# S5 layer: u regrouped through DRAM on GpSimd's queue for state inputs on all 128 rows, tables fetched ten steps ahead, twelve gated outputs accumulated over K

## The chip, the core and the metric

The kernel runs on one core of one Trainium2 chip. The metric is the device time of one execution in microseconds, the median of three runs. All engines, queues and lines are those of that core; L157 is line 157 of the kernel before.

## The reference

A trunk of four layers on x of 256 positions by 1024 channels, float32. Layer i mixes tokens with attention (0, 3), a state-space layer (1) or pooling (2); a SwiGLU feed-forward layer (FFN) follows each. The change lies in the state-space layer, S5:

```python
u = (h @ w_in).astype(F32)
u_g = u.reshape(B, S, S5_GROUPS, S5_GROUP).astype(jnp.complex64)
lam_bar = jnp.exp(lam * dt)
b_bar = ((lam_bar - 1.0) / lam)[..., None] * b_mat
bu = jnp.einsum('gpc,bsgc->bsgp', b_bar, u_g)
_, states = lax.associative_scan(combine, (lam_seq, bu), axis=1)
y = jnp.einsum('gcp,bsgp->bsgc', c_mat, states).real.reshape(B, S, D_MODEL)
y = y + d.astype(F32) * u
g = jax.nn.gelu(y).astype(h.dtype)
val, gate = jnp.split(g @ w_glu, 2, axis=-1)
return val * jax.nn.sigmoid(gate)
```

There are 64 groups of 16 channels with 64 complex states each. `combine` is the first-order recurrence s = lam_bar * s + bu.

## The kernel before

**Dense products.** Activations lie transposed, channels on partitions. Each weight unit of 128 x 1024 is fetched by SyncE (SP) into one of four `raw` buffers, then split into a high and a low float32r part: ScalarE copies (L98), VectorE subtracts (L99), into one of five `hl` buffers. `unit` (L102) hands out the next unit; fetches run three units ahead of use, splits two. A dense product of a unit with 8 k-tiles takes 24 matmuls of 128x256 (`term`, L159: high x high, low x high, high x low), all through `mm` (L157). In the FFN of layers 1 to 3 a pair of matmuls of 512 and 256 columns does the same.

**Ticks.** `tick` (L117) counts the dense work: one tick is about six dense matmuls. Other work is put on ticks with `at` and so lands between dense matmuls. A scheduler then sets the order on each engine; engines run their instructions in that order.

**S5.** `s5` (L780) multiplies eight units of w_s5 (m = 0..7, each one block of 128 channels, that is 8 groups). `evict` (L788) scales a product with the norm R (VectorE, L791) into `u`, whose columns are grouped by position modulo 4. `tables` (L833) fetches, on SP's queue, the block's input matrices E (512 KB), the rotation and decay tables tab (384 KB) and the output matrices par (768 KB) from DRAM, where an earlier stage (`prepare`) has written them on GpSimd's queue (lines L712 to L773). `core` (L843) computes the states of four positions at a time:

```python
for ri in range(2):
    for r in range(4):
        for i in range(4):
            rows = slice(32 * i, 32 * i + 32)
            self.mm(e[:, i, 64 * ri:64 * ri + 64], E[rows, ri, r], u[rows, r], r == 0, r == 3)
```

These are the state inputs: 32 matmuls on 32 rows each (K = 32), four row groups i to four PSUM banks, accumulated over r. Each float32 matmul stands as two instructions on TensorE. VectorE then rotates (products A and B with cosine and sine, L862 to L865), scans (L867), rotates back (L870 to L874) into `sx`. `emit` (L877), six ticks later, adds four feedthrough matmuls of u (`KT`, widths 256, 192, 128, 64) and 32 matmuls of `sx` into the outputs of the block; ScalarE applies gelu (L888), and the result is split into G, high and low (L194, L195). Blocks follow each other every five ticks.

**GLU.** Sixteen output tiles of G @ w_glu: a value and a gate for each of eight column tiles d. Those of d = 0 and 1 are accumulated over k while the blocks run, four 128-column products for each G[k], waiting until block k is emitted. The four banks that `e` used are then opened for the other twelve tiles, whose dense products follow one after the other. Each column is gated (sigmoid on ScalarE, product L829, residual L830) and settled: its next-layer X (ScalarE L209, VectorE L210) and its square (L218, L221).

PSUM has eight banks: two named `acc`, two `tp`, and four in a quad that is either `P` or `e`.

## Time and profile before

| what | value |
|---|---|
| median of three runs | 1142.85 us (1141.98 to 1143.46) |
| the profiled execution | 1147.59 us |
| its span, first to last instruction | 1145.8 us |
| TensorE clock granted in it | 0.995 |
| TensorE, VectorE, ScalarE, GpSimd busy | 97%, 76%, 60%, 11% of the span |
| S5 layer in the span | from 335.56 to 444.62 us |

How to read it. A row of the page or of the groups view names the line, the engine, the operation, the tiles out<-in without buffer numbers, the shape and the count, then the busy time, the mean length of one in ns, and the idle time of the engine ahead of it with what ended it. PE is TensorE's matmul side, PEld its weight loads, DVE VectorE, ACT ScalarE, POOL GpSimd. A timeline row gives start and length in us of neighbouring instructions of one kind. A row of DMA issues gives queue, count, size and the median time from issue to landing. Matmuls are pipelined, so starts tell more of their pace than lengths. A stretches row gives, for each stretch, each engine's busy time and instructions, the granted clock, the share of the DMA engines' time in use, and GB/s.

### The profile page before, as it was taken

How to read it: one execution, taken by the hardware profiler on the slowest of the kernel's cores; microseconds unless marked ns; L12 is line 12 of the kernel's file. 1: busy time of each engine (PE TensorE's matmuls, PEld its weight loads, DVE VectorE, ACT ScalarE, POOL GpSimd, SP SyncE). 2: the span in 40 equal slices, each digit the busy share in tenths (PEclk: the TensorE clock that was granted, in tenths of full speed). 3: DMA queues.
4: the chain of work that ended last, by engine and by line, in shares of the span. 5: the costliest groups of instructions: out<-in, count | busy, mean ns of one | idle time of the engine just before them, and what ended most of it. 6: DMA issues, size and time to landing. Idle time of an engine off the chain costs nothing. (4 is left out here: it accounts for less than half of the span.)

```text
span 1145.8 us, 22375 instructions
## 1 busy us (share of the span) xinstructions
PE 1114.2 (97%) x8706; PEld 1025.4 (89%) x8706; DVE 866.6 (76%) x1647; ACT 682.2 (60%) x1273; POOL 130.1 (11%) x167
## 2 busy tenths in 40 slices
PE   6989999999999999999999899999999999999996
PEld 6888999999999999888888888888899898888886
DVE  6898698887969975988756588876656757878663
ACT  6466675777763254766644676665545777666551
POOL 1187000111110000000000000000004730000000
PEclk9999999999999999999999899999999999999999
DMA  8655366786889744765666255556666544655661
GB/s 267 211 188 164 104 228 224 252 269 213 254 329 332 268 140 155 227 195 186 179 179 194 93 179 194 193 179 189 192 200 215 167 145 148 214 184 188 182 188 49
DMA packets 63210, 224.98 MB, mean 196 GB/s; under 512 B 7648, under 2 KB 7984, under 8 KB 62976
## 3 DMA queue, kind: packets, MB, share of 16 engines
q1 hardware_dynamic: 56368, 200.86, 54.6%
q0 software_dynamic: 6160, 22.00, 5.8%
q8 instruction: 68, 1.11, 0.4%
q10 hardware_dynamic: 576, 0.69, 0.2%
q14 instruction: 38, 0.31, 0.1%
HBM read 208.81 MB, written 14.71 MB: 195 GB/s over the span
## 5 line engine op out<-in xcount | busy, mean ns | idle before, releaser
L157 PE MATMUL P<-X,hl 128*128 128x256 f32 (+1 forms) x4560 | 674.9, 307 | 2.8 <-ACT v L327 1.6
L157 PEld LDWEIGHTS P<-X,hl 128*128 128x128 f32 x4560 | 615.1, 189 | 52.0 <-issue 7.2
L99 DVE TENSOR_TENSOR hl<-raw,hl 128x1024 fp32r<-128x1024 f32 (+3 forms) x363 | 434.5, 1199 | 149.7 <-ACT hl L98 141.7
L98 ACT CAST hl<-raw 128x1024 fp32r<-128x1024 f32 (+3 forms) x363 | 371.7, 1028 | 152.6 <-PE acc L157 71.6
L157 PE MATMUL acc<-H,hl 128*128 128x512 f32 (+1 forms) x1628 | 251.6, 315 | 0.0
L157 PEld LDWEIGHTS acc<-H,hl 128*128 128x128 f32 x1628 | 226.8, 188 | 21.1 <-issue 0.8
L183 ACT COPY lo<-P 128x256 f32<-128x256 f32 x126 | 46.6, 371 | 105.6 <-PE P L157 105.6
L184 DVE TENSOR_TENSOR t<-P,lo 128x256 f32<-128x256 f32 x126 | 53.2, 423 | 44.1 <-ACT lo L183 44.1
L411 POOL TENSOR_SCALAR nb<-nb,c 128x128 f32<-128x128 f32 (+1 forms) x64 | 63.9, 1011 | 1.1
L244 POOL TENSOR_TENSOR rs<-rs,mhalf 128x2 f32<-128x2 f32 x9 | 7.3, 810 | 486.6 <-DVE rs L243 486.6
L157 PE MATMUL acc<-X,hl 128*128 128x256 f32 (+1 forms) x384 | 61.6, 301 | 0.2
L157 PEld LDWEIGHTS acc<-X,hl 128*128 128x128 f32 x384 | 50.6, 188 | 3.9 <-DVE X L195 0.3
L432 ACT ACTIVATE pt<-pt,st 128x128 f32<-128x128 f32 (+1 forms) x64 | 28.6, 447 | 26.0 <-DVE st L430 25.8
L279 ACT ACTIVATE t<-t 128x256 f32<-128x256 f32 x88 | 36.8, 418 | 7.7 <-DVE t L278 4.6
L157 PE MATMUL P<-hl,X 128*128 128x336 f32 (+1 forms) x192 | 40.5, 330 | 0.0
L209 ACT ACTIVATE X<-x,gains 128x256 fp32r<-128x256 f32 x55 | 27.7, 505 | 15.1 <-DVE x L264 14.5
L218 ACT ACTIVATE s<-x 128x256 f32<-128x256 f32 x63 | 25.6, 406 | 15.9 <-DVE x L264 13.1
L157 PEld LDWEIGHTS P<-hl,X 128*128 128x128 f32 x192 | 33.4, 197 | 0.0
L157 PE MATMUL acc<-hl,X 128*128 128x352 f32 x96 | 24.4, 338 | 8.7 <-DVE X L207 7.5
L210 DVE SCALAR_TENSOR_TENSOR X<-x,gains,X 128x256 fp32r<-128x256 f32 x56 | 26.7, 479 | 5.7 <-ACT X L209 5.6
L281 DVE TENSOR_TENSOR t<-t 128x256 f32<-128x256 f32 x66 | 27.9, 423 | 1.8
L278 DVE TENSOR_TENSOR t<-t,R 128x256 f32<-128x256 f32 x66 | 27.9, 423 | 1.8
(179 smaller groups left out, 854.8 us busy)
## 6 DMA issues: line engine op xcount, KB each, us to landing
raw<-in_w_gu SPq DMA_DIRECT2D x176, 512.0 KB, 3.9
raw<-in_w_dn SPq DMA_DIRECT2D x64, 512.0 KB, 3.6
raw<-in_w_qk SPq DMA_DIRECT2D x32, 512.0 KB, 3.4
raw<-in_w_dn SPq DMA_DIRECT2D x32, 384.0 KB, 3.2
raw<-in_w_fo SPq DMA_DIRECT2D x16, 512.0 KB, 4.0
raw<-in_w_glu SPq DMA_DIRECT2D x16, 512.0 KB, 5.8
raw<-in_w_vf SPq DMA_DIRECT2D x15, 520.0 KB, 4.4
nb<-nd POOLq DMA_DIRECT2D x24, 256.0 KB, 5.3
```

The source lines that it names most:

```text
L98: nc.scalar.copy(hl[:, 0, s], raw[:, s])
L99: nc.vector.tensor_tensor(out=hl[:, 1, s], in0=raw[:, s], in1=hl[:, 0, s].bitcast(F32), op=ALU.subtract)
L157: return self.nc.tensor.matmul(out, lhsT=lhsT, rhs=rhs, start=start, stop=stop).ins
L183: nc.scalar.copy(lo, o[:, N:])
L184: nc.vector.tensor_tensor(out=t, in0=o[:, 0:N], in1=lo, op=ALU.add)
L209: nc.scalar.activation(self.X[:, d, 0], x, AF.Identity, scale=g)
L210: nc.vector.scalar_tensor_tensor(out=self.X[:, d, 1], in0=x, scalar=g, in1=self.X[:, d, 0].bitcast(F32), op0=ALU.mult, op1=ALU.subtract)
L278: nc.vector.tensor_tensor(out=t, in0=t if wide else G, in1=R, op=ALU.mult)
L279: nc.scalar.activation(t, t, AF.Silu)
L281: nc.vector.tensor_tensor(out=h, in0=h if wide else U, in1=t, op=ALU.mult)
L411: nc.gpsimd.tensor_scalar(out=nb[:, i], in0=nb[:, i], scalar1=self.c[t][:, 4 * n + i:4 * n + i + 1], scalar2=None, op0=ALU.add)
L432: nc.scalar.activation(pt, pt, AF.Exp, bias=st[:, 0:1], scale=-1.0, accum_out=st[:, 1:2])
```

## The change

1. **State inputs.** u is stored to a DRAM scratch `ud[m]` and loaded back as `ue` by four DMAs, one for each position r modulo 4, all on GpSimd's queue. In `ue` the partitions are (r, c) and the columns (i, j), so all four r stand under each other and one matmul of 128 rows does what four of 32 rows did: 8 matmuls a block, into one `tp` bank. The matrices E are laid out to match (`prepare`: XS).
2. **Rotation.** The tables get a fourth row, minus the sine, made by ScalarE per block; the adds and subtracts on halves become one 512-column add each.
3. **Times.** The core of block m stands at tick 22 + 6m (it was 10 + 5m), and 14 ticks after its eviction at least; its tables are fetched ten ticks ahead; E, tab have three buffers, u eight, ue four. `emit` follows after seven ticks.
4. **GLU.** The quad stays `P`. Twelve of the sixteen output tiles (d = 0 to 5) are accumulated over k in six banks, 36 dense matmuls for each G[k], from sixteen units of 768 columns. Only d = 6 and 7 are left for afterwards, from four units of 1024.

```diff
+FIRST_CORE = 22
...
         def evict(m, P):
-            u = mp.tile([128, 4, 64], F32, tag="u", name="u", bufs=4)
+            u = mp.tile([128, 4, 64], F32, tag="u", name="u", bufs=8)
             nc.vector.tensor_tensor(out=u, in0=v(P), in1=v(self.R), op=ALU.mult)
-            self.at(max(1, 10 + 5 * m - self.now + t0), lambda: self.core(m, u, G))
+            nc.gpsimd.dma_start(self.ud[m], u.rearrange("p r j -> p (r j)"))
+            ue = mp.tile([128, 4, 64], F32, tag="ue", name="ue", bufs=4)
+            def load():
+                for r in range(4):
+                    nc.gpsimd.dma_start(ue[32 * r:32 * r + 32],
+                                      self.ud[m].rearrange("(i c) (r j) -> r c i j", i=4, r=4)[r])
+            load()
+            self.at(max(14, FIRST_CORE + 6 * m - self.now + t0), lambda: self.core(m, u, ue, G))
...
-            self.at(1 + 5 * m, lambda m=m: self.tables(m))
+            self.at(max(1, FIRST_CORE + 6 * m - 10), lambda m=m: self.tables(m))
...
-        acc = [self.bank("acc") for _ in range(2)]
+        outs = [self.bank(t) for t in ("P", "P", "P", "P", "acc", "acc")]
         for k in range(8):
             while self.emitted < k + 1:
                 self.tick()
-            if k % 2 == 0:
+            for h in range(2):
                 hl = self.unit()
-            for d in range(2):
-                for h in range(2):
-                    c = (k % 2 * 4 + 2 * d + h) * 128
-                    self.term(acc[d][:, h * N:h * N + N], hl, slice(c, c + 128), G, k, k == 0 and h == 0, k == 7 and h == 1)
-                self.tick()
-        self.open_quad()
+                for d in range(3):
+                    for s in range(2):
+                        c = (2 * d + s) * 128
+                        self.term(outs[3 * h + d][:, s * N:s * N + N], hl, slice(c, c + 128), G, k,
+                                  k == 0 and s == 0, k == 7 and s == 1)
+                    self.tick()
...
-        e = self.p4.tile([128, 4, 512], F32, tag="e", name="e")
+        nc.scalar.activation(tab[:, 3], tab[:, 1], AF.Identity, scale=-1.0)
+        e = self.bank("tp").rearrange("p (a n) -> p a n", a=2)
         for ri in range(2):
-            for r in range(4):
-                for i in range(4):
-                    rows = slice(32 * i, 32 * i + 32)
-                    self.mm(e[:, i, 64 * ri:64 * ri + 64], E[rows, ri, r], u[rows, r], r == 0, r == 3)
+            for i in range(4):
+                self.mm(e[:, ri, 64 * i:64 * i + 64], E[:, ri, i], ue[:, i], True, True)
...
-        nc.vector.tensor_tensor(out=ij(A), in0=ev, in1=ij(c2), op=ALU.mult)
-        nc.vector.tensor_tensor(out=ij(B), in0=ev, in1=ij(s2), op=ALU.mult)
-        nc.vector.tensor_tensor(out=A[:, 0], in0=A[:, 0], in1=B[:, 1], op=ALU.add)
-        nc.vector.tensor_tensor(out=A[:, 1], in0=A[:, 1], in1=B[:, 0], op=ALU.subtract)
+        nc.vector.tensor_tensor(out=A, in0=e, in1=c2, op=ALU.mult)
+        nc.vector.tensor_tensor(out=B, in0=e[:, ::-1], in1=sn, op=ALU.mult)
+        nc.vector.tensor_tensor(out=A, in0=A, in1=B, op=ALU.add)
...
-        self.at(6, lambda: self.emit(m, u, CX, KT, sx, G))
+        self.at(7, lambda: self.emit(m, u, CX, KT, sx, G))
```

In the order, first TensorE where the first blocks' state inputs stand. P and acc are dense products of w_s5, e<-u,E are state inputs, tp<-u,par the feedthrough. Before:

```order
L157 MATMUL P<-X,hl 128x256 x4
L250 MATMUL tp<-cst,rs 128x128 x2
L157 MATMUL P<-X,hl 128x256 x18
L157 MATMUL acc<-X,hl 128x256 x6
L157 MATMUL e<-u,E 128x64 x32
L157 MATMUL acc<-X,hl 128x256 x13
L157 MATMUL e<-u,E 128x64 x32
L157 MATMUL acc<-X,hl 128x256 x23
```

After (tp<-ue,E are the state inputs):

```order
L158 MATMUL P<-X,hl 128x256 x4
L251 MATMUL tp<-cst,rs 128x128 x2
L158 MATMUL P<-X,hl 128x256 x18
L158 MATMUL acc<-X,hl 128x256 x84
L158 MATMUL tp<-ue,E 128x64 x8
L158 MATMUL acc<-X,hl 128x256 x12
L158 MATMUL tp<-ue,E 128x64 x8
L158 MATMUL acc<-X,hl 128x256 x30
L158 MATMUL tp<-u,par 128x256
```

The state inputs of block 0 stood six dense matmuls after the first two units; now 84 stand between, and 12 dense ones between blocks 0 and 1.

GpSimd's queue from the start of the S5 layer to the next transfer it issues (band, for the pooling layer). Before:

```order
L712 DMA s5d7_88<-pk_2433 128x512
L784 MEMSET sx0_4509 128x8
L784 MEMSET sx1_4510 128x8
L244 TENSOR_TENSOR rs_4504<-rs_4504,mhalf_75 128x2
L472 DMA band_6096<-in_band 128x1088
L474 DMA pbs_6098<-in_pool_bs 128x16
```

After (ud0 and ue_4600 are block 0's, ud1 and ue_4608 block 1's, and so on):

```order
L785 MEMSET sx0_4517 128x8
L785 MEMSET sx1_4518 128x8
L245 TENSOR_TENSOR rs_4512<-rs_4512,mhalf_75 128x2
L793 DMA ud0_81<-u_4597 128x256
L793 DMA ud1_82<-u_4605 128x256
L798 DMA ue_4600<-ud0_81 32x4x64 x4
L798 DMA ue_4608<-ud1_82 32x4x64 x4
L793 DMA ud2_83<-u_4644 128x256
L793 DMA ud3_84<-u_4687 128x256
L793 DMA ud4_85<-u_4732 128x256
L798 DMA ue_4647<-ud2_83 32x4x64 x4
L798 DMA ue_4690<-ud3_84 32x4x64 x4
```

The loads of block 0 stand behind the stores of blocks 0 and 1; those of block 2 behind the stores of blocks 2, 3 and 4.

ScalarE around the first gelu (its output is g, tp its input bank). Before:

```order
L98 CAST hl_4744<-raw_4611 128x1024
L98 CAST hl_4865<-raw_4742 128x1024
L98 CAST hl_4943<-raw_4863 128x1024
L888 ACT_TABLE_LOAD
L888 ACTIVATE g_4802<-tp_4765 128x4x64
L98 CAST hl_5070<-raw_4941 128x1024
L194 CAST X_4513<-g_4802 128x256
L888 ACTIVATE g_4917<-tp_4880 128x4x64
L194 CAST X_4513<-g_4917 128x256
```

After (tab_4593, 4671, 4728 and 4842 are the tables of blocks 0 to 3):

```order
L99 CAST hl_4742<-raw_4697 128x1024
L858 ACTIVATE tab_4671<-tab_4671 128x256
L858 ACTIVATE tab_4728<-tab_4728 128x256
L99 CAST hl_4825<-raw_4740 128x768
L99 CAST hl_4868<-raw_4823 128x768
L99 CAST hl_5021<-raw_4866 128x768
L858 ACTIVATE tab_4842<-tab_4842 128x256
L892 ACT_TABLE_LOAD
L892 ACTIVATE g_4914<-tp_4877 128x4x64
L195 CAST X_4521<-g_4914 128x256
```

The negations of the sine (L858) for blocks 0 to 3 stand ahead of the first gelu, with the splits of GLU units between them.

## The prediction

> **What bounds the kernel now.** I read the page first: it says which engine is busy over the whole span.

> ```profile
> PE 1114.2 (97%) x8706; PEld 1025.4 (89%) x8706; DVE 866.6 (76%) x1647; ACT 682.2 (60%) x1273; POOL 130.1 (11%) x167
> ```

> TensorE is busy all the time. The change touches the S5 layer, so I cut that layer out with the stretches view: its first two dense units, the part in which the eight state blocks run, the last twelve dense units, and ten microseconds of heavy loading.

> ```profile
> core 0: us, PE busy (x) PEld busy (x) DVE busy (x) ACT busy (x) POOL busy (x), PEclk, DMA share, GB/s
> 335.56:342.95 7.39, 6.85 (x56) 6.44 (x55) 3.49 (x8) 2.35 (x5) 0.87 (x3) 1.00 0.85 324
> 342.95:411.57 68.62, 67.39 (x1338) 62.88 (x1337) 60.56 (x107) 22.39 (x30) 0.00 (x0) 1.00 0.75 270
> 411.57:444.62 33.05, 33.05 (x283) 33.05 (x281) 24.98 (x39) 19.63 (x33) 0.00 (x0) 1.00 0.52 176
> 340.00:350.00 10.00, 9.28 (x170) 8.72 (x170) 7.06 (x11) 2.37 (x3) 0.51 (x1) 1.00 0.99 379
> ```

> The layer takes 444.62 - 335.56 = 109.06 us, and TensorE idles in 1.8 us of it. VectorE has 8 us to spare in the middle stretch. The timeline of TensorE gives the price of each piece (start, length, instructions; a length overlaps the next start, so I take start to start):

> ```profile
> 338.90 0.61 PE L157 MATMUL tp<-cst,sq 128*128 128x1 f32 x4
> 339.37 0.72 PE L157 MATMUL P<-X,hl 128*128 128x256 f32 x4
> 340.56 0.43 PE L250 MATMUL tp<-cst,rs 128*128 128x128 f32 x2 [0.47 <-POOL rs L244]
> 342.95 0.87 PE L157 MATMUL acc<-X,hl 128*128 128x256 f32 x6
> 344.06 2.01 PE L157 MATMUL e<-u,E 32*128 32x64 f32 x64 [0.24 <-DVE u L791]
> 346.01 1.81 PE L157 MATMUL acc<-X,hl 128*128 128x256 f32 x13
> 352.50 1.31 PE L157 MATMUL tp<-u,par 128*128 128x256 f32 x8
> 353.75 1.10 PE L157 MATMUL tp<-sx,par 128*32 128x64 f32 x64
> 354.78 0.97 PE L157 MATMUL acc<-X,hl 128*128 128x256 f32 x6
> 360.75 0.65 PE L157 MATMUL tp<-sx,par 128*32 128x64 f32 x30 [0.34 <-issue]
> 386.51 0.53 PE L157 MATMUL tp<-sx,par 128*32 128x64 f32 x19 [0.47 <-issue]
> 411.57 33.21 PE L157 MATMUL P<-X,hl 128*128 128x256 f32 x280
> 444.62 0.87 PE L157 MATMUL acc<-X,hl 128*128 128x512 f32 x4
> 445.33 0.87 PE L157 MATMUL P<-X,hl 128*128 128x512 f32 x4
> ```

> A dense matmul costs 33.05/280 = 0.118 us, so the 576 of the layer (192 of w_s5, 384 of the GLU) cost 68.0. A block's state inputs cost 346.01 - 344.06 = 1.95 (eight: 15.6), its outputs 354.78 - 352.50 = 2.28 (eight: 18.2). With 0.47 for the sums and 0.66 for the spread and its wait that is 102.9 of 109.06. Of the other 6.1 us, 1.05 are the three named idles (0.24, 0.34, 0.47); the rest is small change, some 0.1 us wherever dense and state matmuls meet. So there is little waiting for the change to remove.

> **State inputs on the full array: 0.** Before, 64 instructions stand as 16 groups of four that run side by side on 32 rows each: 1.95/16 = 0.12 us a group. After, 8 matmuls are 16 instructions on 128 rows. Nothing in the trace has their exact shape; two rows bracket it. The sums of squares, four instructions of one column, take 339.37 - 338.90 = 0.47, or 0.117 each, although they move almost nothing; what is left to set that pace is the 128 weight columns that each of them loads. The four feedthrough matmuls (eight instructions, 1280 columns) take 353.75 - 352.50 = 1.25, or 0.00098 a column, which would make 64 columns 0.063. I take 0.117, since every one of the 16 loads new weights: 1.9 us a block, as before. Both ends are kept: 0 or 8 x (1.9 - 1.0) = 7.2 us of gain.

> [...]

> **The regrouping: +0.75.** The first state inputs now need u stored to DRAM, loaded back by four DMAs, all on GpSimd's queue. What hides it is dense work moved ahead: by the order 84 dense matmuls stand before them where six stood, so TensorE reaches them at 342.95 + 84 x 0.118 = 352.86. The other side:

> ```profile
> 342.87 1.14 DVE L791 TENSOR_TENSOR u<-P,R 128x256 f32<-128x256 f32 x2 [3.17 <-PE P L157]
> L712 POOL DMA_DIRECT2D s5d<-pk x3 | 1.6, 540 | 16.2 <-DVE pk L528 16.2
> s5d<-pk POOLq DMA_DIRECT2D x8, 256.0 KB, 3.9
> s5d<-pe POOLq DMA_DIRECT2D x16, 256.0 KB, 4.8
> nb<-nd POOLq DMA_DIRECT2D x24, 256.0 KB, 5.3
> dd<-in_s_d POOLq DMA_DIRECT2D x1, 4.0 KB, 8.1
> out_y<-xg SPq DMA_DIRECT2D x2, 256.0 KB, 2.5
> ```

> u of block 0 is there at about 343.5. Its store (128 KB) should land some 4.3 us later, between the two rows of GpSimd's stores, since the DMA engines are 0.99 busy just then: 347.8. GpSimd spends 0.54 on each issue, so the fourth load starts 3 x 0.54 = 1.6 later, at 349.4. A load of 32 KB in pieces of 256 bytes does not occur before; I take 4.2, nearest to GpSimd's short stores: 353.6. TensorE waits 353.6 - 352.86 = 0.75. The ends: 2.5 for each leg gives 350.1, no wait; 5.3 for each gives 355.7, a wait of 2.9; 8.1, a small load queued behind a large one, gives 361.3, a wait of 8.5. The wait is lost whole, since all dense matmuls of the later units stand behind these on TensorE.

> [...]

> Block 1's loads leave GpSimd about 2.2 us after block 0's, and its matmuls come 1.95 + 12 x 0.118 = 3.4 us after: hidden, with 1.2 us to spare. From block 2 on the loads are done microseconds early. GpSimd has nothing else to do there, so nothing queues behind its waits.

> **The sign table on ScalarE: +0.5.** Each block adds a 256-column negation on ScalarE that needs its table landed, while table buffers are three deep. By the order, block 3's negation stands ahead of the gelu of block 0, and its table may only be fetched when block 0's last multiplication has read its own.

> ```profile
> 346.20 0.68 DVE L862 TENSOR_TENSOR A<-e,tab 128x512 f32<-128x512 f32 x1
> 346.80 0.68 DVE L863 TENSOR_TENSOR B<-e,tab 128x512 f32<-128x512 f32 x1
> L867 DVE TENSOR_TENSOR_SCAN A<-tab,A 128x256 f32<-128x256 f32 x16 | 10.1, 674 | 0.0
> L888 ACT ACT_TABLE_LOAD x1 | 1.3, 1283 | 0.0
> L888 ACT ACTIVATE g<-tp 128x256 f32<-128x256 f32 x8 | 5.1, 635 | 27.5 <-PE tp L157 27.5
> tab<-s5d SPq DMA_DIRECT2D x8, 384.0 KB, 5.7
> par<-s5d SPq DMA_DIRECT2D x8, 768.0 KB, 6.9
> ```

> Counted from the start of block 0's state inputs: 2.1 for them, then on VectorE, 0.6 apart as the two first rows are (346.80 - 346.20), five 512-column operations, two scans, and in between block 1's first product and u of block 5 (0.57, half of the pair above): 2.1 + 8 x 0.6 + 0.6 = 7.5. Fetch 5.7, negation 0.4, table load 1.28, gelu 0.64: 15.5. The outputs of block 1 need the PSUM bank that this gelu empties. TensorE is there after state inputs of block 0, 12 dense matmuls, state inputs of block 1, 30 dense, outputs of block 0, 6 dense, state inputs of block 2, 6 dense, with 0.1 where the kind changes: 1.95 + 1.5 + 1.95 + 3.6 + 2.4 + 0.8 + 2.0 + 0.8 = 15.0. A wait of 0.5. With par's 6.9 it is 1.7; with a table that lands in 4 us, none.

> **Twelve outputs over K, and the end: -0.65 + 0.4 + 0.3.** Between blocks there are now 36 dense matmuls for 30: 36 x 0.118 + 1.95 + 2.28 + 0.3 of changes make 8.8 us a block. VectorE has six 512-column operations and two scans (4.8), G's split (0.4) and two splits of 768 columns (three quarters of the 1.22 below, 1.8): 7.0, so it stays behind TensorE. The wait for u (0.24) goes, and about half of the 0.81 us of "issue" idle, since 48 fewer weight loads and matmuls are issued per block: -0.65. Two blocks' outputs are split round dense work: +0.4. The DMAs of a block are 1.70 MB of tables, 0.79 of weights, 0.26 of u, in 8.8 us 313 GB/s, against the 379 moved at a share of 0.99: hidden, since tables and weights are fetched a block or more ahead; without that lead every block would wait. At the end six columns are settled at once while TensorE has 96 dense matmuls, 11.3 us:

> ```profile
> L99 DVE TENSOR_TENSOR hl<-raw,hl 128x1024 fp32r<-128x1024 f32 x26 | 31.7, 1221 | 7.3 <-ACT hl L98 7.0
> L830 DVE TENSOR_TENSOR x<-x,s 128x256 f32<-128x256 f32 x8 | 3.3, 422 | 0.2
> ```

> VectorE needs 6 x 4 x 0.42 = 10.1 and five splits, 6.1, so 16.2; three columns start up to 3.5 us early, and the FFN asks for the last X only 7/8 of 32 x 0.355 (445.33 - 444.62 holds two pairs) = 9.9 us into it. Only the bank of column 5 is tight: 0 to 1.5, I take 0.3.

> **Sum.** 0 + 0.75 + 0.5 - 0.65 + 0.4 + 0.3 = +1.3 us. The profiled execution took 1147.59 us (span 1145.8, 1.8 around it), so it would take 1148.9. The median of the runs lies 4.7 below that execution, and the difference carries over: 1142.85 + 1.3 = 1144.1.

> **Rivals.** (1) *The round trip is hidden*: both legs land within 3.9 us. Then 1.3 - 0.75 = +0.55, without the sign table's wait +0.05: 1142.9, no change. For it: pk's 3.9. Against: the DMA share of 0.99. [...] (2) *Faster*: the full-array matmuls go at the pace of their columns, 7.2 less: 1136.9. For it: the feedthrough's 0.063; against: 0.117 for one column. [...] (3) *Slower*: the first block's loads queue behind the tables, which in this order are fetched for three blocks in one burst. From 4.75 us a leg on, the wait passes 1.75 and the total 2.3; at 8.1 a leg it is 1.3 + 7.8 = +9: 1151.9; at 6 a leg, +4.9: 1147.7. For it: nb's 5.3 and pe's 4.8; against: a store of half that size, loads of an eighth.

> **Chances.** Below 0.2% (2.3 us) no measurement of this kernel tells a change. The forecast has 0.42, within 1142 to 1146; rival 1 0.18; rival 2 0.10, and 0.02 that all small idles go; rival 3 0.28. Faster is 0.12. Slower is rival 3 and a little of the forecast's upper end, 0.30. The same is the rest, 0.58. The range leaves out rival 2 and the far end of rival 3: 1140.8 to 1148.5.

> **What would show it.** Right: the state-input pieces still take 1.9 us; one wait at the first of them, of 0 to 3 us, named after ue's DMA; a short wait before block 1's feedthrough, named after the gelu; the layer still about 110 us. Wrong: state inputs near 1 us; waits at later blocks; TensorE starved by splits at the start of the FFN.

## The result: slower, and the profile after

The changed kernel takes 1150.61 us (median of 4 runs, 1150.13 to 1151.03); beside it the kernel before took 1143.15 (4 runs). The ratio is 1.0052, 95% interval 1.0036 to 1.0067. In a second series it was 1.0055 (1.0041 to 1.0069). The forecast was 1144.1, with a range to 1148.5.

The lines of the changed kernel lie one higher than before, from L780 on a few more: the matmuls are L158, the eviction of u is L792, the store L793, the loads L798. The profiled execution took 1150.36 us. Its page begins like that of before: TensorE is at work for 97% of the span, only with fewer instructions.

```profile
PE 1114.8 (97%) x8322; PEld 1028.4 (90%) x8322; DVE 866.9 (75%) x1635; ACT 684.0 (60%) x1285; POOL 151.4 (13%) x207
```

So the share of busy time says nothing of the loss. The waits of TensorE in the S5 layer and at the start of the FFN say where it is (engine, line, tile, releaser; total, times, longest):

```profile
PE tp L158 <- DMA ue<-ud: 4.2, 1, 4.2
PE tp L158 <- DVE sq L222: 1.6, 1, 1.6
PE tp L251 <- POOL rs L245: 1.0, 2, 0.6
```

The third was there before. The first two are new. Here are the first state inputs in TensorE's timeline, and a block in the steady part:

```profile
350.73 1.00 PE L158 MATMUL acc<-X,hl 128*128 128x256 f32 x7
355.92 3.65 PE L158 MATMUL tp<-ue,E 128*128 128x64 f32 x16 [4.18 <-DMA ue<-ud]
359.32 2.91 PE L158 MATMUL acc<-X,hl 128*128 128x256 f32 x12
362.03 2.03 PE L158 MATMUL tp<-ue,E 128*128 128x64 f32 x16
...
379.10 1.89 PE L158 MATMUL tp<-ue,E 128*128 128x64 f32 x16
380.80 0.95 PE L158 MATMUL acc<-X,hl 128*128 128x256 f32 x6
```

Two things are to be seen. TensorE stands still for 4.18 us until the first block's `ue` has landed. And then the first block takes 359.32 - 355.92 = 3.40 us where a later one takes 380.80 - 379.10 = 1.70; the twelve dense products behind it take 2.71, where 12 x 0.118 = 1.4. The stretches view tells why: the granted clock is at half for 6.83 us, from just ahead of the end of the wait. The second row is the layer, the third the FFN behind it.

```profile
core 0: us, PE busy (x) PEld busy (x) DVE busy (x) ACT busy (x) POOL busy (x), PEclk, DMA share, GB/s
334.22:444.86 110.64, 105.92 (x1289) 103.49 (x1288) 84.85 (x132) 45.08 (x73) 22.77 (x43) 0.97 0.76 260
444.86:634.40 189.54, 187.39 (x1099) 164.19 (x1098) 138.48 (x221) 110.38 (x187) 1.83 (x3) 1.00 0.60 186
352.06:355.47 3.41, 0.00 (x0) 0.00 (x0) 0.00 (x0) 0.00 (x0) 1.56 (x4) 1.00 0.89 278
355.47:362.30 6.83, 6.38 (x30) 6.41 (x31) 2.01 (x4) 1.66 (x2) 5.72 (x11) 0.50 0.52 138
```

How long the legs of the round trip took stands in the DMA issues from 342 to 352.9 us (size, median us from issue to landing). The DMA share there is 1.02, and the weights beside them need 12.4 us:

```profile
raw<-in_w_glu SPq DMA_DIRECT2D x2, 384.0 KB, 12.4
ud<-u POOLq DMA_DIRECT2D x2, 128.0 KB, 6.0
ue<-ud POOLq DMA_DIRECT2D x8, 32.0 KB, 5.4
```

The second wait is on VectorE's account. In its timeline at the start of the FFN it stands still for 2.34 us ahead of a product of 128x8, the pooling bias and scale of layer 2, whose table comes over GpSimd's queue. X and squares of the columns d = 6 and 7 are behind it, and so the sums:

```profile
448.51 0.43 DVE L839 TENSOR_TENSOR x<-x,s 128x256 f32<-128x256 f32 x1
451.27 0.17 DVE L476 TENSOR_TENSOR pbs<-pbs 128x8 f32<-128x8 f32 x1 [2.34 <-DMA pbs<-in_pool_bs]
451.36 0.48 DVE L211 SCALAR_TENSOR_TENSOR X<-x,gains,X 128x256 fp32r<-128x256 f32 x1
```

### The profile page after: what moved, and what is told of

Read it like the earlier page. It is cut to its first block, busy times and chain, and to the rows that moved or that the text cites. A ratio compares the mean times of both kernels' runs of the same rounds, so it can differ in the third digit from the quotient of the medians.

```text
span 1148.6 us, 21710 instructions
## 1 busy us (share of the span) xinstructions
PE 1114.8 (97%) x8322; PEld 1028.4 (90%) x8322; DVE 866.9 (75%) x1635; ACT 684.0 (60%) x1285; POOL 151.4 (13%) x207
## 5 line engine op out<-in xcount | busy, mean ns | idle before, releaser
L158 PE MATMUL P<-X,hl 128*128 128x256 f32 (+1 forms) x4512 | 672.1, 308 | 1.3 <-ACT y L504 1.3
L158 PEld LDWEIGHTS P<-X,hl 128*128 128x128 f32 x4512 | 611.7, 189 | 50.1 <-issue 7.2
L100 DVE TENSOR_TENSOR hl<-raw,hl 128x1024 fp32r<-128x1024 f32 (+3 forms) x367 | 435.8, 1190 | 145.7 <-ACT hl L99 137.5
L99 ACT CAST hl<-raw 128x1024 fp32r<-128x1024 f32 (+3 forms) x367 | 372.7, 1020 | 158.3 <-PE acc L158 57.2
L158 PE MATMUL acc<-H,hl 128*128 128x512 f32 (+1 forms) x1628 | 251.5, 315 | 0.0
L158 PEld LDWEIGHTS acc<-H,hl 128*128 128x128 f32 x1628 | 226.7, 188 | 21.1 <-issue 0.8
L158 PE MATMUL acc<-X,hl 128*128 128x256 f32 (+1 forms) x384 | 63.4, 305 | 0.0
L158 PEld LDWEIGHTS acc<-X,hl 128*128 128x128 f32 x384 | 52.1, 193 | 2.9 <-DVE s L838 0.3
L158 PE MATMUL P<-hl,X 128*128 128x336 f32 (+1 forms) x192 | 40.4, 329 | 0.0
L210 ACT ACTIVATE X<-x,gains 128x256 fp32r<-128x256 f32 x55 | 27.7, 505 | 20.8 <-DVE x L265 15.5
L158 PE MATMUL acc<-hl,X 128*128 128x352 f32 x96 | 24.4, 338 | 9.1 <-DVE X L208 7.4
L158 PEld LDWEIGHTS P<-hl,X 128*128 128x128 f32 x192 | 33.2, 196 | 0.0
## 6 DMA issues: line engine op xcount, KB each, us to landing
raw<-in_w_dn SPq DMA_DIRECT2D x32, 384.0 KB, 3.2
nb<-nd POOLq DMA_DIRECT2D x24, 256.0 KB, 5.6
par<-s5d SPq DMA_DIRECT2D x8, 768.0 KB, 6.5
```

Of the source, the lines that this page charges most:

```text
L99: nc.scalar.copy(hl[:, 0, s], raw[:, s])
L100: nc.vector.tensor_tensor(out=hl[:, 1, s], in0=raw[:, s], in1=hl[:, 0, s].bitcast(F32), op=ALU.subtract)
L158: return self.nc.tensor.matmul(out, lhsT=lhsT, rhs=rhs, start=start, stop=stop).ins
L210: nc.scalar.activation(self.X[:, d, 0], x, AF.Identity, scale=g)
```

## The experiments

The theory (A): the round trip of u costs its wait, and the half clock that follows on the wait; the pool product costs the rest; all else in the change is a gain. Rivals: B, the layer gives such a wait back before it ends; C and G, the half clock comes by itself, against F, it comes after an idle stretch of over about 2 us, and H, after any; D and E, on why the legs are long. (In pbs_pool alone, B stands for something else: that the six columns settled at once are late by VectorE's own work.) Each kernel is measured beside the kernel before on its chip. "S5" and "FFN" are the lengths of the layer and of the FFN behind it in the profiled execution.

| kernel | median us (runs) | ratio, 95% interval | S5 | FFN |
|---|---|---|---|---|
| before, again | 1143.15 (1) | | 108.11 | 187.59 |
| changed | 1150.61 (4) | 1.0052, 1.0036 to 1.0067 | 110.64 | 189.54 |
| changed, again | 1151.00 (6) | 1.0055, 1.0041 to 1.0069 | 111.14 | 189.39 |
| pbs_pool | 1147.79 (12) | 1.0027, 1.0016 to 1.0038 | 110.42 | 187.66 |
| filler | 1150.88 (7) | 1.0058, 1.0037 to 1.0080 | 109.71 | 189.06 |
| core30 | 1161.82 (5) | 1.0153, 1.0132 to 1.0175 | 121.95 | 190.24 |
| no_trip | 1140.03 (5) | 0.9955, 0.9942 to 0.9968 | 103.27 | 187.73 |
| two_sets | 1144.75 (12) | 1.0006, 0.9994 to 1.0018 | 109.03 | 187.63 |
| legs_act | 1150.08 (6) | 1.0048, 1.0035 to 1.0061 | 113.37 | 187.70 |
| quad | 1140.58 (6) | 0.9962, 0.9950 to 0.9975 | 103.36 | 187.78 |
| hold19 | 1145.06 (11) | 1.0012, 1.0001 to 1.0024 | 110.77 | 187.70 |
| hold23 | 1150.45 (6) | 1.0052, 1.0039 to 1.0065 | 114.68 | 187.65 |
| hold30 | 1155.18 (4) | 1.0091, 1.0076 to 1.0105 | 118.31 | 187.64 |

### The kernel before, once more

> The kernel before, once more, for a second profile. The profiled execution of the first (1147.59 us) lay 4.4 above the median of its runs, that of the changed kernel (1150.36) on its median, so the two traces are only 2.8 us apart where the medians are 7.5 apart. Theory A (the loss lies in the mixer of layer 1 and the start of its FFN) expects an execution near 1143.2 us in which the stretch from the first sums of layer 1 to the FFN after it is 104 to 106 us, against 109.1 in the first trace and 110.6 in the changed kernel. The rival (a profile costs this kernel 4 us anywhere) expects 1147 to 1148 us again, and 109 us there.

The execution took 1143.15 us, as A said, but the stretch did not come out at 104 to 106: S5 is 108.11 us here and 109.06 in the first trace. Most of the 4.4 us between the two executions lies in layer 0 (from its first sums to those of its FFN: 117.6 and 114.1 us), which the change doesn't touch. The two rows to compare with:

```profile
333.15:441.26 108.11, 106.85 (x1672) 102.25 (x1671) 89.16 (x153) 44.41 (x66) 0.87 (x3) 1.00 0.70 247
441.26:628.85 187.59, 187.15 (x1099) 164.36 (x1098) 135.14 (x211) 108.60 (x182) 1.83 (x3) 1.00 0.60 188
```

So the loss in the traces is 110.64 - 108.11 = 2.5 us in S5 and 189.54 - 187.59 = 1.95 in the FFN, 4.5 of the 6 to 7.5 us between the medians. The rest lies outside these two stretches: 1.1 us ahead of them and 1.6 behind.

### The pool product off VectorE: pbs_pool

```diff
-        nc.vector.tensor_tensor(out=self.pbs[:, 16:24], in0=self.pbs[:, 0:8], in1=self.pbs[:, 8:16], op=ALU.mult)
+        nc.gpsimd.tensor_tensor(out=self.pbs[:, 16:24], in0=self.pbs[:, 0:8], in1=self.pbs[:, 8:16], op=ALU.mult)
```

> The changed kernel, with one instruction on another engine: the product of the pooling bias and scale (line 476) on GpSimd, so that VectorE doesn't stand in its order waiting for the pool table. Theory A: the wait of 1.59 us of the sums at the start of the FFN falls under 0.2, and the time from 1150.6 to about 1149.0 (ratio to the kernel before about 1.0038); the wait at the first state inputs stays at about 4.2. Theory B (the loss is the tail: six columns are settled at once and VectorE is late there by its own work): the sums wait as long as before, 1150.6 (1.0052).

One instruction on another engine, and 2.8 us are gone (1.9 of them in the FFN of the trace, 189.54 to 187.66). TensorE's waits from 430 to 460 us are down to the one that the kernel always had:

```profile
PE tp L251 <- POOL rs L245: 0.6, 1, 0.6
```

So the B of this run falls: the six columns settled at once don't hold up the sums, the foreign instruction among them did. The gain is larger than the 1.6 us that A expected, in the median more than in the trace; why is not shown. S5 is as long as before the edit (110.42). All kernels below but filler and core30 carry it.

### TensorE kept busy through the wait: filler

```diff
         e = self.bank("tp").rearrange("p (a n) -> p a n", a=2)
+        for n in range(36 if m == 0 else 0): self.mm(e[:, 0], self.X[:, n % 8, 0, 0:128], self.X[:, n % 8, 0], True, True)
```

> The changed kernel with 36 more matmuls of 128x128 by 128x256 ahead of the state inputs of block 0, into the bank that the state inputs overwrite, so that TensorE works (36 x 0.117 = 4.2 us) where it stood idle for 4.18. Theory A (the idle stretch is what brings the clock down to half for 6.8 us): the clock stays at full speed around the state inputs of block 0, they take 1.7 us instead of 3.4 and the dense products behind them 1.5 instead of 2.7; 3.0 us less in all, 1147.6 (ratio 1.0026). Theory C (the half clock comes at that place whatever TensorE did just ahead): the half clock is still there, 1150.6 or more. Theory B (what is lost here is given back before the layer ends): 1150.6 and no half clock.

The timeline of TensorE there:

```profile
350.65 4.48 PE L158 MATMUL tp<-X 128*128 128x256 f32 x36
356.40 1.97 PE L158 MATMUL tp<-ue,E 128*128 128x64 f32 x16 [1.28 <-DMA ue<-ud]
358.18 1.67 PE L158 MATMUL acc<-X,hl 128*128 128x256 f32 x12
```

In the trace the half clock is gone: the block takes 358.18 - 356.40 = 1.78, the dense products behind it 1.5. That speaks for A and against C. But the loads took 4.9 to 6.9 us here, so 1.28 us of wait stay, and S5 is shorter by 0.9 only. The median is that of the changed kernel, not the 1147.6 that A expected, with executions from 1146.1 (the profiled one) to 1154.6. What the others did isn't in the trace; as a measurement of time this one is inconclusive.

### The first blocks later: core30

```diff
-FIRST_CORE = 22
+FIRST_CORE = 30
```

> The changed kernel with FIRST_CORE at 30: 24 more dense products (24 x 0.117 = 2.8 us) stand ahead of the first state inputs. Theory A: the wait there falls from 4.18 to about 1.4 us and the half clock goes: 2.8 + 3.0 less, 1144.8 us (ratio 1.0015), or 1147.8 (1.0027) if 1.4 us of idle still bring it; up to 1 us of that may come back as a wait at the first outputs, which now follow closer on the state inputs. Theory B (given back before the layer ends): 1150.6 (1.0052).

The timeline of TensorE at the first block, and at the first gated products:

```profile
355.85 1.97 PE L158 MATMUL tp<-ue,E 128*128 128x64 f32 x16 [1.88 <-DMA ue<-ud]
...
364.99 1.10 PE L158 MATMUL tp<-sx,par 128*32 128x64 f32 x64
369.61 2.08 PE L158 MATMUL P<-X,hl 128*128 128x256 f32 x8 [3.51 <-ACT X L195]
```

A miss. The wait falls, from 4.18 to 1.88 where about 1.4 was expected, and the clock stays whole there. But the gated products of G[k] now come right behind the outputs of block k, and wait for gelu and split: 3.51 us at the first block and 1.18 at each of six later ones, 10.6 in all; on the 3.51 follow 3.41 us of half clock (369.40 to 372.81). The steps between a block and its use were needed. Starting the blocks later costs more than it hides as long as the gated products stay where they are; moving these along was not tried.

### No round trip: no_trip

```diff
-            nc.gpsimd.dma_start(self.ud[m], u.rearrange("p r j -> p (r j)"))
...
-            load()
+            ue = u
```

> The changed kernel with the pool product on GpSimd (1147.8 us so far, ratio 1.0027) and without the round trip: nothing is stored to or loaded from DRAM, and the state inputs read u as it lies, so that what leaves out the regrouping is the computation itself: the states are made from rows in the wrong places. Theory A (the round trip of blocks 0 and 1 costs its wait and the half clock behind it): the wait of 4.2 to 4.5 us at the first state inputs goes and with it the half clock that cost about 3.4; 1140.2 us (0.9961), faster than the kernel before. Theory B (the layer gives it back further on): 1147.8. Theory C (the half clock comes at that place anyway): 1143.4 (0.9989).

The first state inputs in the timeline, and the layer in the stretches view:

```profile
351.12 1.90 PE L158 MATMUL tp<-u,E 128*128 128x64 f32 x16
352.83 1.68 PE L158 MATMUL acc<-X,hl 128*128 128x256 f32 x12
```

```profile
333.77:437.04 103.27, 102.73 (x1289) 100.48 (x1287) 84.56 (x132) 45.23 (x73) 0.87 (x3) 1.00 0.73 258
```

1140.03 us where A said 1140.2. No wait, no half clock, and S5 is 110.42 - 103.27 = 7.2 us shorter than in pbs_pool. B and C are out. It also gives the worth of the rest of the change: 103.27 against 108.11, a gain of 4.8.

### Why the legs are long: two_sets and legs_act

```diff
-        E = mp.tile([128, 2, 4, 128], F32, tag="E", name="E", bufs=3)
+        E = mp.tile([128, 2, 4, 128], F32, tag="E", name="E", bufs=2)
...
-        tab = mp.tile([128, 4, 256], F32, tag="tab", name="tab", bufs=3)
+        tab = mp.tile([128, 4, 256], F32, tag="tab", name="tab", bufs=2)
```

> The changed kernel with the pool product on GpSimd, and E and tab in two buffers again as in the kernel before, so that the third block's state-input and rotation tables (0.9 of the 5 MB that are queued while u makes its round trip) are asked for only when block 0 is done. Theory D (the legs of the round trip take 5.2 to 6.3 us because they share the DMA engines with the burst of tables): the legs fall to 4 to 5 us, the wait at the first state inputs to 2 to 3 us, the time to about 1145 (1.0005), or 1146 if the half clock stays. Theory E (a leg on GpSimd's queue takes this long whatever else is on its way): legs and wait as before, 1147.8 (1.0027).

In the DMA issues of two_sets from 342 to 353 us the stores are still at 6.5, the loads, which land as the burst runs out, at 3.9:

```profile
ud<-u POOLq DMA_DIRECT2D x2, 128.0 KB, 6.5
ue<-ud POOLq DMA_DIRECT2D x8, 32.0 KB, 3.9
```

The wait is 3.24 us, and the half clock behind it 3.41 instead of 6.83. The time, 1144.75 us, is what D said. Of the legs only the loads came out as D said, while the stores kept their length, so this run alone doesn't decide.

```diff
-            nc.gpsimd.dma_start(self.ud[m], ...)
+            (nc.scalar if m < 2 else nc.gpsimd).dma_start(self.ud[m], ...)
...
-                    nc.gpsimd.dma_start(ue[32 * r:32 * r + 32],
+                    (nc.scalar if m < 2 else nc.gpsimd).dma_start(ue[32 * r:32 * r + 32],
```

> The changed kernel with the pool product on GpSimd, and both legs of blocks 0 and 1 issued by ScalarE instead of GpSimd (the other six blocks as they were). Theory E: the legs are at least 1.5 us shorter each and the wait at the first state inputs falls from 4.2 to about 1; 1144.5 us less about 3 if the half clock goes too (1.0000 to 0.997). Theory D: through the same busy DMA engines the legs take 5 to 6 us as before, the issues (0.55 us each on GpSimd, 0.3 to 0.4 on SyncE) save 0.7 us, the wait is about 3.5 and the half clock stays; 1147 (1.002). Either way ScalarE stands still for the first leg, and the casts behind it come that much later: if a dense product waits for them, up to 3 us more.

The same kernel shows both cases. Its DMA issues, first from 342 to 350.35 us, the stretch in which SyncE issues one transfer only:

```profile
E<-s5d SPq DMA_DIRECT2D x1, 512.0 KB, 5.0
ud<-u ACTq DMA_DIRECT2D x2, 128.0 KB, 6.0
ud<-u POOLq DMA_DIRECT2D x2, 128.0 KB, 3.0
ue<-ud ACTq DMA_DIRECT2D x4, 32.0 KB, 1.9
```

The stores that ScalarE issues into the burst take 6.0 us, as long as GpSimd's did. The loads of block 0, issued at 348.45 to 349.78, find the DMA engines less busy (their share is 0.59 from 348.45 to 350.36, 1.01 ahead of it) and take 1.9. From 350.36 to 362 SyncE issues again, and the loads of block 1 on the same queue, and GpSimd's, take three times as long:

```profile
raw<-in_w_glu SPq DMA_DIRECT2D x3, 384.0 KB, 9.6
...
ue<-ud POOLq DMA_DIRECT2D x8, 32.0 KB, 7.2
...
ue<-ud ACTq DMA_DIRECT2D x4, 32.0 KB, 5.9
```

So D holds in this: what else is on its way sets the length of a leg here (1.9 or 5.9 us for loads of 32 KB on one queue, ScalarE's), whichever engine issues it; E falls. The time, 1150.08, was missed by both, since neither saw block 1. Block 0 doesn't wait any more, but block 1 does, for 5.87 us until 361.16: its last load landed at 360.96. Nothing is won. The cast behind ScalarE's wait came 7.7 us late, and no dense product waited for it.

### Regrouped in SBUF: quad

```diff
-            nc.gpsimd.dma_start(self.ud[m], u.rearrange("p r j -> p (r j)"))
...
-                for r in range(4):
-                    nc.gpsimd.dma_start(ue[32 * r:32 * r + 32],
-                                      self.ud[m].rearrange("(i c) (r j) -> r c i j", i=4, r=4)[r])
+                for n in range(16):
+                    r, i = n // 4, n % 4
+                    nc.gpsimd.tensor_copy(ue[32 * r:32 * r + 32, i], u[32 * i:32 * i + 32, r])
```

> The changed kernel with the pool product on GpSimd, and the regrouping done in SBUF: 16 copies of 32x64 a block on GpSimd, from one quarter of the partitions to another, in the place of one store and four loads. Nothing in the traces shows such a copy; GpSimd's nearest rows are 0.12 us (a memset of 128x8) and 0.72 us (the power of 128x2). At 0.2 us a copy block 0 is regrouped 3.2 us after u, where TensorE comes for it 9.2 us after, and the time is that without a round trip: 1140.2 us (0.9961) by theory A, 1147.8 by theory B. At over 0.52 us a copy the regrouping falls behind the blocks (one every 8.4 us) and the kernel is slower than now.

The copies in the groups view, and the first state inputs in the timeline:

```profile
L799 POOL COPY ue<-u 32x64 f32<-32x64 f32 x128 | 55.9, 437 | 8.8 <-DVE u L792 3.0
```

```profile
351.11 1.90 PE L158 MATMUL tp<-ue,E 128*128 128x64 f32 x16
352.81 1.68 PE L158 MATMUL acc<-X,hl 128*128 128x256 f32 x12
```

A copy takes 0.437 us in the mean, so 7.0 a block of 8.4: near the bound that was named, but kept. TensorE never waits for it, and 1140.58 us is the time without a round trip. This version leaves nothing out, and is faster than both kernels, by 0.4% than the one before.

### What an idle stretch costs: hold19, hold23, hold30, and the changed kernel again

```diff
-                    nc.gpsimd.tensor_copy(ue[32 * r:32 * r + 32, i], u[32 * i:32 * i + 32, r])
+                    (nc.scalar.copy if m == 1 else nc.gpsimd.tensor_copy)(ue[32 * r:32 * r + 32, i], u[32 * i:32 * i + 32, r])
...
+                for n in range(19 if m == 0 else 0): nc.gpsimd.tensor_copy(ue[0:32, 0], u[0:32, n % 4])
```

> The changed kernel once more, with a second profile and more runs beside the other three. All theories: 1150 us beside a kernel before of 1144 (1.0052), a wait of 4.2 to 4.5 us at the first state inputs and a wait of 1.6 us at the start of the FFN. Theory F (the granted clock is set for stretches of 3.41 us, and goes to half after a stretch in which TensorE stood idle for over about 2 us): a half clock of 3.41 or 6.83 us begins between 1 us ahead of the end of the long wait and 3 us behind it. Theory G (it comes by itself, at random): it may lack here.

> The kernel that regroups in SBUF by copies (quad, 1140.6 us, ratio 0.9962), with 19 more copies on GpSimd ahead of block 0's, which do nothing but hold its state inputs back, and block 1's copies on ScalarE. From the rows of quad a copy comes every 0.27 us, block 0's are done at 347.2 and TensorE comes at 351.1: 19 x 0.27 = 5.1 gives an idle stretch of about 1.3 us. Theory F: too short for the half clock; 1140.6 + 1.3 = 1141.9 (0.9973). Theory H (any idle stretch at this place costs the half clock): 1.3 + 3.0 = 1144.9 (1.0000). Theory G: as F.

> As hold19 with 23 copies: an idle stretch of about 2.4 us. Theory F: where it falls whole into one stretch of 3.41 us, a half clock of 3.41 us behind it (1.7 us), otherwise none; a mixture of 1143.0 and 1144.7 (0.9983 to 0.9998), differing from execution to execution. Theory G: 1143.0 always.

> As hold19 with 30 copies: an idle stretch of about 4.2 us, as long as the wait of the changed kernel, with no transfer in it. Theory F: always a half clock of 3.41 or 6.83 us behind it; 4.2 + 1.7 to 3.4 more than quad, 1146.5 to 1148.2 (1.0013 to 1.0028). Theory G: 1144.8 (0.9999).

My idle stretches came out longer than planned: 2.42, 4.77 and 9.88 us for 1.3, 2.4 and 4.2. Some copies take over 1 us (up to 1.15 in quad; block 0's end at 348.85 in quad, not at 347.2), and in hold23 and hold30 the scheduler put copies of a later block between the last of the extra ones (16 of them from 357.23 to 363.85 us in hold30), behind which block 0's last copy stands. So the times that were expected are missed, and what there is to test is the sum. The first state inputs of hold19 in the timeline, and the half clock of hold30 in the stretches view (7.72 us of it with TensorE at work):

```profile
354.89 3.20 PE L158 MATMUL tp<-ue,E 128*128 128x64 f32 x16 [2.42 <-POOL ue L800]
```

```profile
358.54:372.19 13.65, 7.72 (x36) 7.72 (x37) 3.32 (x6) 0.00 (x0) 11.47 (x47) 0.50 0.20 68
```

Take 103.3 us (no_trip, quad), add the idle stretches, and half of the time for which TensorE works at half clock:

| kernel | wait at ue | other new idle | half clock, of it at work | sum | S5 measured |
|---|---|---|---|---|---|
| two_sets | 3.24 | 0.59 | 3.41, 3.41 | 108.8 | 109.03 |
| changed | 4.18 | | 6.83, 6.38 | 110.7 | 110.64 |
| changed, again | 4.07 | | 6.83, 6.83 | 110.8 | 111.14 |
| pbs_pool | 4.47 | | 6.83, 5.40 | 110.5 | 110.42 |
| legs_act | 5.87 | | 10.24, 8.01 | 113.2 | 113.37 |
| hold19 | 2.42 | 0.66, 0.67 | 6.83, 6.83 | 110.5 | 110.77 |
| hold23 | 4.77 | 0.66 | 13.65, 11.92 | 114.7 | 114.68 |
| hold30 | 9.88 | 0.66, 0.39 | 13.65, 7.72 | 118.1 | 118.31 |

Every row closes within 0.4 us, with no transfer of u in the last three. filler and core30, which change TensorE's order itself, are not in the table; for core30 such a sum stays 4.6 us short of its 121.95. An idle stretch of 2.4 us or more at the first two blocks has brought the half clock in all eight traces that have one; the 1.28 us of filler and the 1.88 of core30 have not. H, that any idle stretch costs it, falls with these two. G, by chance, can be left: 8 of 8 against 0 of 6 (before twice, filler, core30, no_trip, quad) at the same place.

These are single executions, and 2.42 us is the shortest of the eight. hold19's trace (1148.00 us) is that of the slowest of its 11 runs; six of them took 1142.4 to 1145.1, and 1140.6 + 2.4 + 1.3 = 1144.3 is the time without a half clock at this place. That fits a half clock in some executions only, as theory F has it for a stretch of about this length, but times alone don't show it.

## Why the prediction was wrong, step by step

- **State inputs on the full array, 0: wrong, to the good side.** A block takes 1.70 us (380.80 - 379.10), 0.106 an instruction, against the 0.117 that I took from the sums of squares. 8 x 0.25 is 2.0 us won.
- **The regrouping, +0.75: this step failed.** The mechanism and the place were right: one wait, at the first state inputs, named after ue's DMA. The legs were mis-sized. I gave the store 4.3 us, the load 4.2; they took 5.8 (block 0's store, 342.43 to 348.22) and 5.5 (its fourth load). The prices were medians of GpSimd's stores over stretches that had less on the way in the mean. The right one stood in the trace of before: the three of pe's stores that ran at a DMA share of 0.95 or more (issued at 294.25, 313.25 and 326.20) took 5.4 to 5.7. I had named the DMA share of 0.99 and the burst of tables for three blocks, and given them a chance of 0.28 in rival 3 only, because the loads are an eighth in size. legs_act shows that size is no shelter: loads of 32 KB took 1.9 us at a DMA share of 0.59 and 5.9 to 7.2 behind 384 to 768 KB pieces. The page's medians, over all places, are not the price at one place.
- **No term for the clock.** The wait itself, 4.18, lies inside the ends that I gave (0 to 8.5). What no end held is the half clock after it: 6.38/2 = 3.2 us. So rival 3 was the right case with too low a price; with 5.5 to 6 us a leg it gave up to 1147.7.
- **The end, +0.3: mis-sized.** It was 1.95 us, and not by "six columns settled at once": an instruction of the pooling layer stands among them in VectorE's order and waits 2.34 us for a small transfer (pbs_pool). In the order before it stood behind the sums, where its wait cost nothing. I had not looked for instructions that have nothing to do with the change.
- **The sign table, +0.5: not seen.** No wait stands ahead of block 1's outputs, and S5 has no other new one.
- **Removed idles, -0.65: about right.** They are 0.7 us. Two outputs split round dense work, +0.4: not seen; the outputs of `sx` take 8.25 us in all instead of 8.66, and the dense products 0.122 each instead of 0.124, 1.1 in all.

The layer in sum, start to start over all its matmuls, no_trip against the second trace of before: -2.3 state inputs (13.63 for 15.97), -1.1 dense, -0.7 outputs, -0.7 idles. With the changed kernel's +4.2 wait and +3.2 half clock that makes +2.6; measured +2.5. So the layer is still about 110 us, which I had named as a sign of being right, but by errors that offset each other.

With 1.95 in the FFN this is 4.5 of the 6 to 7.5 us. In the ratios of the medians the pool product is worth 0.0028 (changed, again, against pbs_pool), the round trip 0.0072 (pbs_pool against no_trip) and all else a gain of 0.0045 (no_trip against the kernel before), which is the whole 0.0055. Why the medians show more than the traces was not settled. The 1.6 us behind the FFN are a longer half clock ahead of layer 2, 6.83 us (638.78 to 645.61) where the second trace of before has 3.41 (634.64 to 638.05); but its first trace has 6.83 too, so this differs between executions of one kernel. The mean granted clock of the changed kernel's runs is 0.988, that of the kernel before 0.994, of quad 0.994; 0.006 of 1149 us is 6.9, so more half clock is at hand than the one in S5, but only the profiled executions show where, and there the others stand in layers 0 and 2 and at the end, in both kernels.

## What to carry to other kernels

A wait of TensorE costs its length and, in the eight traces with 2.42 to 9.88 us of idle time at the first two blocks, half a clock for 3.41 us or more behind it, where 1.28 and 1.88 us brought none: count both. A transfer's price is read where it will run, with what is queued there, not from the median of its kind: loads of 32 KB took a median of 1.9 to 7.2 us within legs_act alone. Where data only change partitions, copies on an idle engine need no queue: quad's took 7.0 us a block, and TensorE waited for none. When an order moves, look also for the instructions that have nothing to do with the change but wait for something themselves.

## What the runs showed of the hardware

```profile
79.00:82.41 3.41, 3.41 (x18) 3.41 (x17) 2.77 (x16) 3.14 (x12) 3.41 (x5) 0.50 0.64 207
...
638.78:645.61 6.83, 6.83 (x32) 6.83 (x33) 1.45 (x3) 2.25 (x6) 0.00 (x0) 0.50 0.14 58
```

With the start at 355.47 shown above, 355.47 - 79.00 = 276.47 is 81.0 steps, 638.78 - 355.47 = 283.31 is 83.0. In the second trace of before the starts at 78.27 and 634.64 are 163.0 steps apart. An idle stretch of 2.24 us stands in layer 0 of the changed kernel and of the first trace of before. In the changed kernel it lies whole in one step, and the half clock from 79.00 follows. In the trace of before the border of a step cuts it (78.95, 163.0 steps ahead of the half clock that starts at 635.33), and none follows. Here are the changed kernel's step, the two of before, and the step of hold19's wait, which half clock follows from 355.44 to 362.27; the length less PE's busy time is the idle time:

```profile
75.58:79.00 3.42, 1.18 (x10) 0.94 (x10) 3.42 (x8) 1.31 (x4) 2.47 (x2) 1.00 0.34 105
...
75.54:78.95 3.41, 2.72 (x26) 1.90 (x24) 3.34 (x13) 3.07 (x8) 1.30 (x1) 1.00 0.20 73
78.95:82.37 3.42, 1.83 (x16) 1.83 (x17) 2.88 (x13) 1.40 (x7) 3.32 (x4) 1.00 0.65 175
...
352.03:355.44 3.41, 0.99 (x9) 0.78 (x7) 0.00 (x0) 1.66 (x2) 2.77 (x13) 1.00 0.02 6
```

In these two traces, from 16 us after the start to 1130 us, the steps at full clock with 2.24 and 3.41 us of idle time are followed by half clock (75.58 and 352.06 in the changed kernel). So are those with 1.67 and 1.73 ahead of layer 2 (631.91 in before, 635.37 in the changed kernel). Five with 1.03 to 1.59 are not, and none with less is. core30's wait of 1.88 brought none; what decides there is open. Nor is it shown why the 2.42 us of hold19 brought 6.83 us at half clock and the 2.24 in layer 0 of the changed kernel 3.41.

**Some of GpSimd's copies take longer.** In a stretch of hold30 in which VectorE does nothing, 37 copies of 32x64 take 8.04 us, 0.22 each:

```profile
354.60:364.47 9.87, 0.00 (x0) 0.00 (x0) 0.00 (x0) 1.66 (x2) 8.04 (x37) 0.70 0.00 2
```

In quad they take 0.23 to 1.15, 0.437 in the mean. Its first ones run while VectorE subtracts in SBUF (L100):

```profile
341.74 5.15 POOL L799 COPY ue<-u 32x64 f32<-32x64 f32 x9 [3.04 <-DVE u L792]
...
342.13 2.39 DVE L100 TENSOR_TENSOR hl<-raw,hl 128x1024 fp32r<-128x1024 f32 x2
```

Nine copies take 5.15 us here, 0.57 each. VectorE's two operations take 1.2 each, as in the kernel before (1.22 in the mean). That VectorE's work is the cause is not shown. Block 0's copies in quad are done 2.3 us before TensorE comes (348.85 and 351.11), so it costs nothing there; in hold19 TensorE waits 2.42 us for a copy.
